# Softmax weights of eleven heads transposed by VectorE in 32x32 blocks by way of HBM, in place of TensorE

## The chip, the cores and the metric

One core of a Trainium2 chip. The time is device microseconds from the first to the last instruction of one launch, the median of several runs. Lower is better. TensorE is PE (its weight loads PEld), VectorE DVE, ScalarE ACT, GpSimd POOL, SyncE SP, whose queue issues most of the DMAs.

## The reference, cut to what matters

A block of an encoder on 256 tokens of width 2048: twelve attention heads beside a Fourier mixer, an output projection, and a gated feed-forward part, all in fp32.

```python
h = _rmsnorm(x, norm1_g)
proj = h @ w_in                       # q: 12 heads x 128, k and v: 4 x 128, u: 512
...
scores = jnp.einsum('bnqkgd,bnskd->bnkgqs', qb, kb).astype(jnp.float32)
scores = scores * (HEAD_DIM ** -0.5)
...
m = jnp.maximum(jnp.max(scores, axis=-1, keepdims=True), sink_b)
p = jnp.exp(scores - m)
p = p / (jnp.sum(p, axis=-1, keepdims=True) + jnp.exp(sink_b - m))
out = jnp.einsum('bnkgqs,bnskd->bnqkgd', p.astype(v.dtype), vb)
...
x = x + jnp.concatenate([a, f], axis=-1) @ w_out
x = x + _conv_ffn(_rmsnorm(x, norm2_g), w_up, dw_w, dw_b, w_down)
```

The sum over the keys `s` in the last einsum wants the softmax weights `p` with keys on the partitions. The scores come out with queries on the partitions. In between stands a transposition of 128 queries x 256 keys, twice (there are two blocks of 128 queries), for each head.

## The kernel before

**Units.** Weights arrive in units of 1 MB (128 partitions x 2048 fp32). Units 0 to 3 are the Fourier input, 4 to 7 the values (`v_hi`, `v_lo`), 8 to 23 the keys and queries in the order k0 q0 q1 q2 k1 q3 q4 q5 k2 ... (`QK_ORDER`), 24 to 39 the output projection, and then the feed-forward weights. Each fp32 operand is split into a rounded part and the rest (`hi`, `lo`), and a product is made of three matmuls hi x hi, lo x hi, hi x lo. So a weight is prepared by two instructions: ACT writes `hi` (`split`, L185), then DVE writes `lo` = raw - hi (L186).

**The order of the work** is written out by hand. Every engine runs its own queue in program order. A unit `i` issues, in this order: the small jobs listed in `before` (on PE, ahead of the projection), the projection of unit `i`, the jobs listed in `beside`, the split of unit `i + 2` with the load of unit `i + 5` on SP (the raw buffers are three, so a load waits until the split has freed one), and the jobs listed in `behind`. So on DVE and ACT the `beside` jobs of unit `i` stand between the split of unit `i + 1` and that of unit `i + 2`.

**A head through the units.** If query `h` is projected in unit `s`, then its sum leaves PSUM in `s + 1` (`qk_out`: ACT copies one half to `tmp`, DVE adds; `qk_parts`: ACT rounds into `qT`, DVE takes the rest). The scores are made by PE at the start of unit `s + 2` (`scores`), DVE adds the distance bias and finds the maximum (`scores_out`), and ACT takes the exponentials behind the split (`exps`). In `s + 3` DVE divides by the sums (`weigh`, L702 to L706). At the start of `s + 4` PE transposes four 128x128 blocks into PSUM (`turn`, L713), and ACT and DVE split the result into `pt0`, `pt1` (`turn_out`, L725, L726). At the start of `s + 5` PE multiplies by the values (`values`, L735), and `values_out` squares and scales the result into `cat` (`feature_out`, L492 and `split_scaled`, L234, L235), while POOL sums the squares.

Every fourth projection is a key, so in a round of four units each of these steps comes three times, and which unit lacks it depends on the step. The `beside` jobs of a unit before:

```python
        for kind, h in new:
            if kind == "q":
                at(beside, i, lambda k=kind, h=h: qk_out(k, h, st.pop(("ps", k, h))))
        if 4 in heads:
            at(beside, i, turn_out, heads[4])
        if 3 in heads:
            at(beside, i, weigh, heads[3])
```

and then the key's `qk_out`, `qk_parts`, `scores_out` and `values_out`. `heads[d]` is the head whose query was projected `d` units ago. In units 9 to 13 the four Fourier groups pass through the same engines (`fourier_channels` and what follows it); they use four buffers with the tag `sc`, which the scores take over.

Of the kernel before, what the change touches and what calls it, by code (L numbers as in the profile page):

```python
# [8 lines left out]
F32 = mybir.dt.float32  # L9
F32R = mybir.dt.float32r  # L10
AF = mybir.ActivationFunctionType
ALU = mybir.AluOpType

P = 128
D = 2048
S = 256
NK = D // P
HD = 128
NH = 12
# [32 lines left out]
N_OUT = N_QK + len(QK_ORDER)  # L52
# [44 lines left out]
def block_kernel(  # L97
# [18 lines left out]
    nc = tc.nc  # L116
# [4 lines left out]
    dram = ctx.enter_context(tc.tile_pool(name="dram", bufs=1, space=bass.MemoryType.DRAM))  # L121
    mm = ctx.enter_context(tc.tile_pool(name="mm", bufs=4, space=bass.MemoryType.PSUM))
    dn = ctx.enter_context(tc.tile_pool(name="dn", bufs=4, space=bass.MemoryType.PSUM))

    def f32(ap):
        return ap.bitcast(F32)
# [13 lines left out]
    def bank(pool, name):  # L140
        return pool.tile([P, 512], F32, tag=pool.name, name=name)
# [63 lines left out]
    for n, size in enumerate(U_LOADS[1:], 1):  # L205
        k = sum(U_LOADS[:n])
# [15 lines left out]
    ident = base.tile([P, P], F32, tag="ident", name="ident")  # L222
    make_identity(nc, ident)

    ps = bank(dn, "ps_warm")
# [21 lines left out]
    for c in range(4):  # L247
        t = base.tile([P, 4, 512], F32R, tag=f"hT{c}", name=f"hT{c}")
# [45 lines left out]
    k = 0  # L294
# [15 lines left out]
    ph = pa.enter_context(tc.tile_pool(name="pa", bufs=1))  # L310
# [103 lines left out]
    before, beside, behind = {}, {}, {}  # L414

    def at(when, i, f, *a):
        when.setdefault(i, []).append((f, a))
# [136 lines left out]

    def fourier_rows_out():
        for g in range(NG):
            t = ph.tile([P, 512], F32, tag="sc", name=f"uf{g}", bufs=4)[:, 0:S]
            if g % 2:
                nc.scalar.activation(t, held.pop(("f", g))[:, 0:S], AF.Copy)
            else:  # L560
                nc.vector.tensor_copy(t, held.pop(("f", g))[:, 0:S])
            us.append(t)
# [39 lines left out]
    at(beside, 8, fourier_weights_out)  # L602
    at(before, 7, fourier_rows)
    at(beside, 7, fourier_rows_out)
    at(beside, 8, lambda: rows_out(v_hi, v_lo, ps_v))
    at(behind, 8, distances)
# [23 lines left out]
    qk_sb, st = {}, {}  # L630
    sq_a = ph.tile([P, S], F32, tag="sq", name="sq_a")

    def qk_out(kind, h, ps):
        tmp = ph.tile([P, S], F32, tag="tmp", name=f"tmp_{kind}{h}", bufs=2)
        nc.scalar.activation(tmp, ps[:, S : 2 * S], AF.Copy)
        add = ph.tile([P, S], F32, tag="add", name=f"add_{kind}{h}", bufs=2)
        nc.vector.tensor_tensor(add, ps[:, 0:S], tmp, ALU.add)
        if kind == "k":
            nc.vector.tensor_tensor(add, add, r1b, ALU.mult)
        st["add", kind, h] = add  # L640
# [30 lines left out]
    def scores_out(h):  # L671

        ps = st.pop(("s", h))
        sc = ph.tile([P, 512], F32, tag="sc", name=f"sc{h}", bufs=4)
        mx = ph.tile([P, 2], F32, tag="mx", name=f"mx{h}", bufs=2)
        neg = ph.tile([P, 2], F32, tag="neg", name=f"neg{h}", bufs=2)
        for b in range(2):
            s = slice(b * S, (b + 1) * S)
            nc.vector.tensor_tensor_reduce(
                sc[:, s], ps[:, s], rel[:, s], -float(SL[h]), -3e38, ALU.add,  # L680
                ALU.max, mx[:, b : b + 1],
            )
        nc.vector.tensor_tensor(neg, mx, rq_neg, ALU.mult)
        nc.vector.tensor_scalar(neg, neg, sink_neg[:, h : h + 1], None, ALU.min)
        st["sc", h] = sc, neg
# [20 lines left out]
            nc.vector.tensor_scalar(sc[:, s], sc[:, s], ex[:, b : b + 1], None, ALU.mult)  # L706

    def turn(h):
        ps = st["t", h] = bank(dn, f"ps_t{h}")
        sc = st.pop(("sc", h))[0]  # L710
        for sb in range(2):
            for b in range(2):
                nc.tensor.transpose(  # L713
                    ps[:, b * S + sb * P : b * S + (sb + 1) * P],
                    sc[:, b * S + sb * P : b * S + (sb + 1) * P],
                    ident,
                )

    def turn_out(h):
        ps = st.pop(("t", h))  # L720
        pt = [
            ph.tile([P, 512], F32R, tag=f"pt{q}", name=f"pt{q}{h}", bufs=2)
            for q in range(2)
        ]
        nc.scalar.activation(pt[0], ps, AF.Copy)  # L725
        nc.vector.tensor_tensor(pt[1], ps, f32(pt[0]), ALU.subtract)  # L726
        st["p", h] = pt
# [21 lines left out]
    for i in range(N_QK, N_OUT + 8):  # L749
        heads = {i - s: h for (kind, h), s in slot_of.items() if kind == "q"}  # L750
        new = [kh for kh, s in slot_of.items() if i - s == 1]
        if i - 9 in range(NG):
            at(before, i, fourier_channels, i - 9)
        if 5 in heads:
            at(before, i, values, heads[5], mm if i < N_OUT else dn)
        if 4 in heads:
            at(before, i, turn, heads[4])
        if i == 15:
            at(before, i, total, sq_f, "f")
        if 2 in heads:  # L760
            at(before, i, scores, heads[2])

        for kind, h in new:
            if kind == "q":
                at(beside, i, lambda k=kind, h=h: qk_out(k, h, st.pop(("ps", k, h))))
        if 4 in heads:
            at(beside, i, turn_out, heads[4])
        if 3 in heads:
            at(beside, i, weigh, heads[3])
        for kind, h in new:  # L770
            if kind == "k":
                at(beside, i, lambda k=kind, h=h: qk_out(k, h, st.pop(("ps", k, h))))
            at(beside, i, qk_parts, kind, h)
        if 2 in heads:
            at(beside, i, scores_out, heads[2])
            at(behind, i, exps, heads[2])
        if 5 in heads:
            at(beside, i, values_out, heads[5])

    fourier_channels_steps()  # L780
    for n, (kind, h) in enumerate(QK_ORDER):
# [57 lines left out]
    for n, (c, kq) in enumerate(OUT_ORDER):  # L839
        i = N_OUT + n  # L840
# [14 lines left out]
        if kq >= 2:  # L855
            part = "a" if kq == 2 else "f"
            ps = ps_a[c] if kq < 3 else ps_a[c, "f"]
            last = c in added
# [306 lines left out]
    for q in range(2):  # L1165
        kind, j = items[q]
        ps = bank(mm, f"ps_{kind}{j}")
# [16 lines left out]
    for n, it in enumerate(items):  # L1184
# [8 lines left out]
        if it[0] in ("gate", "val"):  # L1193
            kind, j = it
            ps = bank(mm, f"ps_{kind}{j}")
# [4 lines left out]
        if it[0] == "product":  # L1200
            kind, g, c, p = it
            hi, lo = halves.pop(it)
            both = c == 2
            shape = (2, 1024) if both else (4, 512)
            for cc in (0, 1) if both else (c,):
                o = 512 * cc if both else 0
# [4 lines left out]
                ps = bank(mm, f"ps_{p}{g}{cc}")  # L1211
# [6 lines left out]
        else:  # L1218
            kind, g, c = it
            hi, lo = halves.pop(up_index[n])  # L1220
            ps = [bank(mm, f"ps_l{g}{c}{b}") for b in range(2)]
# [10 lines left out]
    i = up_index[n]  # L1232
# [156 lines left out]
```

## Time and profile before

| | |
|---|---|
| median of three runs | 905.73 us (905.62 to 905.91) |
| the profiled execution | 905.91 us, of which the span shown is 904.1 us |
| PE, PEld busy | 895.6 us, 808.5 us |
| DVE, ACT, POOL busy | 746.0 us, 546.7 us, 51.6 us |
| transposes of the softmax weights on PE (`ps_t`) | 48 matmuls of 128x128, 80.4 to 173.2 us |
| DMA | 214.86 MB, mean 238 GB/s |

The span is cut into instructions by engine. A timeline row reads: start in us, length in us, engine, line, operation, output <- inputs, partitions x elements and type, how many were joined into the row, and in brackets how long the engine had been idle and which instruction on which engine ended that. Names stand without their numbers. On PE, lengths overlap, because matmuls are pipelined: what one costs is read from the start of one to the start of the next. A row of the stretches view reads: the stretch, its length, then for each engine busy time and number of instructions, the granted clock of PE, the DMA engines' mean share and GB/s.

### The profile page before, as it was taken

The numbers are of one execution on the slowest core, as the hardware profiler recorded it, in microseconds if no ns is written. First come the engines' busy times: TensorE is split into PE (matmuls) and PEld (weight loads), VectorE is DVE, ScalarE is ACT, GpSimd is POOL, SyncE is SP. The second block draws the span as 40 slices with busy tenths as digits, with TensorE's granted clock in tenths as the row PEclk, the third lists the DMA queues.
The fourth block names the chain that finished last, engine by engine and source line by source line (L and its number), as shares of the span: only waits on it lengthen the run. The fifth ranks groups of instructions, "written<-read, shape, count | busy, mean of one in ns | idle before, by whom it ended". The sixth has DMA issues, their size and how long they took to land.

```text
span 904.1 us, 12736 instructions
## 1 busy us (share of the span) xinstructions
PE 895.6 (99%) x5064; PEld 808.5 (89%) x5064; DVE 746.0 (83%) x894; ACT 546.7 (60%) x661; POOL 51.6 (6%) x65
## 2 busy tenths in 40 slices
PE   9999999999999999999999999999999999999996
PEld 7899999888899999999999999999999999999885
DVE  7569888666668877889887998878988789998996
ACT  7757677555455656556565565566655566656544
POOL 0001111000000000000000000000000000000004
PEclk9999999999999999999999999999999999999999
DMA  9964544456568678677898779887888988779652
GB/s 359 343 232 142 187 155 171 145 182 227 192 242 272 231 242 252 187 256 235 271 265 271 245 258 285 261 278 238 274 250 244 312 263 263 242 240 289 213 198 94
DMA packets 32908, 214.86 MB, mean 238 GB/s; under 512 B 3632, under 2 KB 4016, under 8 KB 8528
## 3 DMA queue, kind: packets, MB, share of 16 engines
q1 hardware_dynamic: 28592, 184.29, 54.9%
q0 software_dynamic: 4112, 29.49, 17.5%
q8 instruction: 40, 0.66, 0.3%
q10 hardware_dynamic: 144, 0.26, 0.1%
q14 instruction: 20, 0.16, 0.0%
HBM read 211.93 MB, written 2.10 MB: 237 GB/s over the span
## 4 chain that ended last, share of the span: by engine, by line
PE 95%; DVE 2%; POOL 1%; issue 1%; ACT 0%; POOLq 0%; ACTq 0%; DVEq 0%
PE ps_val L395 17%; PE ps_gate L395 17%; PE ps_gate L397 8%; PE ps_val L397 8%; PE ps_q L395 5%; PE ps_P L1106 3%; PE ps_P L1108 3%; PE ps_P L1107 3%; PE ps_N L1106 2%; PE ps_N L1108 2%; PE ps_N L1107 2%; PE ps_u L289 2%; PE ps_q L397 2%; PE ps_a L378 2%; PE ps_a L380 2%; PE ps_a L379 2%
## 5 line engine op out<-in xcount | busy, mean ns | idle before, releaser
L186 DVE TENSOR_TENSOR parts<-raw,parts 128x2048 fp32r<-128x2048 f32 (+1 forms) x129 | 293.2, 2273 | 47.1 <-ACT parts L185 46.4
L185 ACT ACTIVATE parts<-raw 128x2048 fp32r<-128x2048 f32 (+1 forms) x129 | 245.6, 1903 | 44.5 <-PE ps_a L380 12.4
L395 PE MATMUL ps_val<-hU,parts 128*128 128x512 f32 x688 | 227.7, 382 | 0.0
L395 PE MATMUL ps_gate<-hU,parts 128*128 128x512 f32 x688 | 227.3, 382 | 0.0
L397 PE MATMUL ps_val<-hU,parts 128*128 128x256 f32 x688 | 187.5, 273 | 0.0
L397 PE MATMUL ps_gate<-hU,parts 128*128 128x256 f32 x688 | 186.9, 273 | 0.0
L395 PEld LDWEIGHTS ps_val<-hU,parts 128*128 128x128 f32 x688 | 130.0, 189 | 18.1
L395 PEld LDWEIGHTS ps_gate<-hU,parts 128*128 128x128 f32 x688 | 130.0, 189 | 18.1
L397 PEld LDWEIGHTS ps_val<-hU,parts 128*128 128x128 f32 x688 | 132.0, 192 | 0.8
L397 PEld LDWEIGHTS ps_gate<-hU,parts 128*128 128x128 f32 x688 | 131.8, 192 | 0.9
L884 ACT ACTIVATE ft_g<-ps_gate 128x256 f32<-128x256 f32 x43 | 16.5, 384 | 112.5 <-PE ps_gate L397 109.9
L395 PE MATMUL ps_q<-hT,parts 128*128 128x512 f32 x192 | 62.6, 384 | 0.0
L884 ACT ACTIVATE ft_v<-ps_val 128x256 f32<-128x256 f32 x43 | 16.5, 384 | 73.4 <-PE ps_val L397 73.4
L1106 PE MATMUL ps_P<-parts_P,op_P 128*128 128x512 f32 x144 | 54.7, 380 | 0.0
L1107 PE MATMUL ps_P<-parts_P,op_P 128*128 128x512 f32 x144 | 54.6, 379 | 0.0
L1108 PE MATMUL ps_P<-parts_P,op_P 128*128 128x512 f32 x144 | 54.6, 379 | 0.0
L397 PE MATMUL ps_q<-hT,parts 128*128 128x256 f32 x192 | 50.4, 273 | 0.0
L992 DVE TENSOR_TENSOR parts_N<-sumw,parts_N 128x2048 fp32r<-128x2048 f32 x18 | 41.2, 2288 | 9.9 <-ACT parts_N L991 9.9
L1106 PE MATMUL ps_N<-parts_N,op_N 128*128 128x512 f32 x108 | 41.0, 380 | 0.0
L1107 PE MATMUL ps_N<-parts_N,op_N 128*128 128x512 f32 x108 | 40.9, 379 | 0.0
L1108 PE MATMUL ps_N<-parts_N,op_N 128*128 128x512 f32 x108 | 40.9, 379 | 0.0
L395 PEld LDWEIGHTS ps_q<-hT,parts 128*128 128x128 f32 x192 | 36.1, 189 | 4.7
(344 smaller groups left out, 1555.0 us busy)
## 6 DMA issues: line engine op xcount, KB each, us to landing
raw<-in_w_up SPq DMA_DIRECT2D x86, 1024.0 KB, 6.2
raw<-in_w_in SPq DMA_DIRECT2D x20, 1024.0 KB, 4.9
sumw<-in_w_down POOLq DMA_DIRECT2D x18, 1024.0 KB, 8.4
raw<-in_w_out SPq DMA_DIRECT2D x16, 1024.0 KB, 4.8
raw<-in_w_down_late SPq DMA_DIRECT2D x4, 1024.0 KB, 5.3
u_raw<-in_u_in SPq DMA_DIRECT2D x4, 768.0 KB, 10.9
raw<-in_w_down_last SPq DMA_DIRECT2D x4, 768.0 KB, 4.2
u_raw<-in_u_in SPq DMA_DIRECT2D x7, 384.0 KB, 6.4
```

The costliest lines, as they stand in the source:

```text
L185: nc.scalar.activation(hi, raw, AF.Copy)
L186: nc.vector.tensor_tensor(lo, raw, f32(hi), ALU.subtract)
L289: nc.tensor.matmul(ps_u[b], block(hk(k), part, b, True), in_turn(w), start=k == 0 and n == 0, stop=k == NK - 1 and n == 2,)
L378: nc.tensor.matmul(ps, ah, wh, start=first and q == q0, stop=False)
L379: nc.tensor.matmul(ps, al, wh, start=False, stop=False)
L395: nc.tensor.matmul(ps, hi[:, s], in_turn(h), start=k == 0, stop=False)
L397: nc.tensor.matmul(ps[:, 0:S], lo[:, s], in_turn(h)[:, 0:P], start=False, stop=k == NK - 1)
L884: nc.scalar.activation(tmp, ps[:, S : 2 * S], AF.Copy)
L992: nc.vector.tensor_tensor(lo, src, f32(hi), ALU.subtract)
L1106: nc.tensor.matmul(ps, o[:, 0, p, :], wh, start=first and p == 0, stop=False)
L1107: nc.tensor.matmul(ps, o[:, 1, p, :], wh, start=False, stop=False)
L1108: nc.tensor.matmul(ps, o[:, 0, p, :], wl, start=False, stop=end)
```

## The change

Head 11 keeps its way. For heads 0 to 10 the four transposes on PE are replaced:

- `turn(h)`, now in unit `s + 3` directly behind `weigh(h)`: one DVE instruction transposes all 32x32 blocks of the 128x512 weights within their partitions' groups of 32, with the blocks regrouped in the output (`tb`); SP writes the result to a tensor in HBM.
- `fetch(h)`, in `s + 4`: four DMAs on SP read it back, each into 32 partitions, which brings every block to the partitions it belongs to (`td`).
- `turn_out(h)`, in `s + 5`, now the last of the `beside` jobs: ACT and DVE split `td` (in SBUF, not PSUM) into `pt0`, `pt1`.
- `values(h)` in `s + 6` and not `s + 5`.

`weigh` moves ahead of the query's `qk_out`. The buffers with the tag `sc` go from four to one; the room goes to `tb` (one) and `td` (two), and the Fourier groups' four buffers are spread over these.

```diff
-            t = ph.tile([P, 512], F32, tag="sc", name=f"uf{g}", bufs=4)[:, 0:S]
+            tag, bufs = [("sc", 1), ("tb", 1), ("td", 2), ("td", 2)][g]
+            t = ph.tile([P, 512], F32, tag=tag, name=f"uf{g}", bufs=bufs)[:, 0:S]
...
-        sc = ph.tile([P, 512], F32, tag="sc", name=f"sc{h}", bufs=4)
+        sc = ph.tile([P, 512], F32, tag="sc", name=f"sc{h}", bufs=1)
...
     def turn(h):
+        sc = st.pop(("sc", h))[0]
+        t = ph.tile([P, 512], F32, tag="tb", name=f"tb{h}", bufs=1)
+        nc.vector.transpose(
+            t.rearrange("p (k n e) -> p n k e", k=4, e=32),
+            sc.rearrange("p (n k e) -> p n k e", k=4, e=32),
+        )
+        st["h", h] = dram.tile([P, 512], F32, tag=f"turn{h}", name=f"turn{h}")
+        nc.sync.dma_start(st["h", h], t)
+
+    def fetch(h):
+        d = st["t", h] = ph.tile([P, 512], F32, tag="td", name=f"td{h}", bufs=2)
+        t = st.pop(("h", h))
+        for k in range(4):
+            nc.sync.dma_start(
+                d[32 * k : 32 * (k + 1), :].rearrange("r (a e) -> r a e", a=4),
+                t[:, P * k : P * (k + 1)].rearrange("(a r) e -> r a e", r=32),
+            )
+
+    def turn_out(h):
+        d = st.pop(("t", h)).rearrange("p (a n e) -> p n a e", a=4, e=32)
...
+        hi, lo = (t.rearrange("p (n a e) -> p n a e", a=4, e=32) for t in pt)
+        nc.scalar.activation(hi, d, AF.Copy)
+        nc.vector.tensor_tensor(lo, d, f32(hi), ALU.subtract)
...
-        if 5 in heads:
-            at(before, i, values, heads[5], mm if i < N_OUT else dn)
-        if 4 in heads:
-            at(before, i, turn, heads[4])
+        valued = [h for d, h in heads.items() if d == (5 if h == NH - 1 else 6)]
+        for h in valued:
+            at(before, i, values, h, mm if i < N_OUT else dn)
+        turned = {d: h for d, h in heads.items() if h < NH - 1}
+        last = {d: h for d, h in heads.items() if h == NH - 1}
...
+        if 4 in turned:
+            at(beside, i, fetch, turned[4])
+        if 3 in heads:
+            at(beside, i, weigh, heads[3])
+        if 3 in turned:
+            at(beside, i, turn, turned[3])
 
         for kind, h in new:
             if kind == "q":
                 at(beside, i, lambda k=kind, h=h: qk_out(k, h, st.pop(("ps", k, h))))
-        if 4 in heads:
-            at(beside, i, turn_out, heads[4])
-        if 3 in heads:
-            at(beside, i, weigh, heads[3])
...
-        if 5 in heads:
-            at(beside, i, values_out, heads[5])
+        for h in valued:
+            at(beside, i, values_out, h)
+        if 5 in turned:
+            at(beside, i, turn_out, turned[5])
```

How this stands in the engines' queues is shown for unit 18, in which query 6 is finished and head 5 weighed. The names carry their head or unit (the figures behind the underscore are buffer numbers). On DVE, from the split of unit 19 to that of unit 20, before:

```order
L186 TENSOR_TENSOR parts19_1249<-raw19_1005,parts19_1249 128x2048
L637 TENSOR_TENSOR add_q6_1306<-ps_q6_1193,tmp_q6_1304 128x256
L726 TENSOR_TENSOR pt14_1309<-ps_t4_1266,pt04_1308 128x512
L702 TENSOR_TENSOR sm5_1254<-sm5_1254,ex5_1255 128x2
L703 RECIPROCAL ex5_1255<-sm5_1254 128x2
L706 TENSOR_SCALAR sc5_1242<-sc5_1242,ex5_1255 128x256 x2
L235 SCALAR_TENSOR_TENSOR qT6_1316<-add_q6_1306,qT6_1316 128x256
L235 SCALAR_TENSOR_TENSOR cat3_1321<-ps_o3_1259,vec_88,cat3_1321 128x256
L186 TENSOR_TENSOR parts20_1325<-raw20_1093,parts20_1325 128x2048
```

and with the change:

```order
L186 TENSOR_TENSOR parts19_1265<-raw19_1002,parts19_1265 128x2048
L704 TENSOR_TENSOR sm5_1270<-sm5_1270,ex5_1271 128x2
L705 RECIPROCAL ex5_1271<-sm5_1270 128x2
L708 TENSOR_SCALAR sc5_1252<-sc5_1252,ex5_1271 128x256 x2
L715 STREAM_TRANSPOSE tb5_1317<-sc5_1252 128x4x4x32
L639 TENSOR_TENSOR add_q6_1323<-ps_q6_1198,tmp_q6_1321 128x256
L235 SCALAR_TENSOR_TENSOR qT6_1325<-add_q6_1323,qT6_1325 128x256
L740 TENSOR_TENSOR pt13_1329<-td3_1231,pt03_1328 128x512
L186 TENSOR_TENSOR parts20_1332<-raw20_1088,parts20_1332 128x2048
```

Weighing and the new transposition now stand ahead of the query's add, and the softmax parts, of head 3 and not head 4, have gone from behind the add to the place ahead of the next split. On ACT in the same unit, before:

```order
L635 ACTIVATE tmp_q6_1304<-ps_q6_1193 128x256
L725 ACTIVATE pt04_1308<-ps_t4_1266 128x512
L234 ACTIVATE qT6_1316<-add_q6_1306 128x256
L492 ACTIVATE sq3_1319<-ps_o3_1259 128x256
L234 ACTIVATE cat3_1321<-ps_o3_1259,vec_88 128x256
L185 ACTIVATE parts20_1325<-raw20_1093 128x2048
```

and with the change:

```order
L637 ACTIVATE tmp_q6_1321<-ps_q6_1198 128x256
L234 ACTIVATE qT6_1325<-add_q6_1323 128x256
L739 ACTIVATE pt03_1328<-td3_1231 128x512
L185 ACTIVATE parts20_1332<-raw20_1088 128x2048
L637 ACTIVATE tmp_q7_1389<-ps_q7_1275 128x256
```

ACT's half of the softmax parts (`pt0`) has moved from ahead of the query to between the query and the split. The values of head 3 are not in this unit any more; they are made a unit later. On SP, from the load of unit 21 to that of unit 24, where before there were only the loads:

```order
L177 DMA raw21_1177<-in_w_in 128x2048
L726 DMA td3_1231<-turn3_1148 32x4x128 x4
L720 DMA turn4_1242<-tb4_1240 128x512
L177 DMA raw22_1268<-in_w_in 128x2048
L726 DMA td4_1308<-turn4_1242 32x4x128 x4
L720 DMA turn5_1319<-tb5_1317 128x512
L177 DMA raw23_1335<-in_w_in 128x2048
L726 DMA td5_1384<-turn5_1319 32x4x128 x4
L177 DMA raw24_1416<-in_w_out 128x2048
```

Between two loads stand the four reads of one head and the write of the next.

More of the change, by code (lines that the diff above doesn't have):

```diff
@@ L708, in turn, with turn_last @@
     def turn(h):
+        sc = st.pop(("sc", h))[0]
[16 more added lines that the diff above has]
+        d = st.pop(("t", h)).rearrange("p (a n e) -> p n a e", a=4, e=32)
+        pt = [
+            ph.tile([P, 512], F32R, tag=f"pt{q}", name=f"pt{q}{h}", bufs=2)
+            for q in range(2)
+        ]
+        hi, lo = (t.rearrange("p (n a e) -> p n a e", a=4, e=32) for t in pt)
+        nc.scalar.activation(hi, d, AF.Copy)
+        nc.vector.tensor_tensor(lo, d, f32(hi), ALU.subtract)
+        st["p", h] = pt
+    def turn_last(h):
         ps = st["t", h] = bank(dn, f"ps_t{h}")
@@ L712, in turn, with turn_last_out @@
             for b in range(2):
[L713 to L719, printed above, removed]
+                o = b * S + sb * P
+                nc.tensor.transpose(ps[:, o : o + P], sc[:, o : o + P], ident)
+    def turn_last_out(h):
         ps = st.pop(("t", h))
@@ L753, in block_kernel @@
             at(before, i, fourier_channels, i - 9)
-        if 5 in heads:
-            at(before, i, values, heads[5], mm if i < N_OUT else dn)
-        if 4 in heads:
-            at(before, i, turn, heads[4])
+        valued = [h for d, h in heads.items() if d == (5 if h == NH - 1 else 6)]
[3 more added lines that the diff above has]
+        last = {d: h for d, h in heads.items() if h == NH - 1}
+        if 4 in last:
+            at(before, i, turn_last, last[4])
         if i == 15:
@@ L765, in block_kernel @@
                 at(beside, i, lambda k=kind, h=h: qk_out(k, h, st.pop(("ps", k, h))))
-        if 4 in heads:
-            at(beside, i, turn_out, heads[4])
-        if 3 in heads:
-            at(beside, i, weigh, heads[3])
+        if 4 in last:
+            at(beside, i, turn_last_out, last[4])
         for kind, h in new:
```

## The prediction

> **What bounds the kernel now.** I read the engine shares first, then the chain of work that ended last, then the waits of PE.
>
> ```profile
> PE 895.6 (99%) x5064; PEld 808.5 (89%) x5064; DVE 746.0 (83%) x894; ACT 546.7 (60%) x661; POOL 51.6 (6%) x65
> PE 95%; DVE 2%; POOL 1%; issue 1%; ACT 0%; POOLq 0%; ACTq 0%; DVEq 0%
> PE ps_warm L229 <- PEq L1379: 0.8, 1, 0.8
> ```
>
> PE is busy throughout, carries 95% of the chain, and waited once, at the start. So an instruction taken from PE is worth its whole length, and a wait put on PE costs its whole length. The change touches the units of queries and keys. The stretches view gives one round of four there, units 18 to 21 on PE. DVE and ACT finish in a unit what PE projected in the unit before, here three queries and a key.
>
> ```profile
> 113.47:139.76 26.29, 26.29 (x178) 24.61 (x177) 22.41 (x49) 18.71 (x37) 2.46 (x3) 1.00 0.46 160
> ```
>
> The round is 26.29 us, PE full, DVE busy 22.41, ACT 18.71, the granted clock 1.00.
>
> **What the change takes from PE.** The timeline of PE shows the units' first instructions.
>
> ```profile
> 93.08 0.39 PE L735 MATMUL ps_o<-pt,v_hi 128*128 128x256 f32 x2
> ...
> 113.47 0.39 PE L735 MATMUL ps_o<-pt,v_hi 128*128 128x256 f32 x2
> ...
> 114.14 0.60 PE L713 MATMUL ps_t<-ident,sc 128*128 128x128 f32 x4
> 114.50 1.33 PE L395 MATMUL ps_q<-hT,parts 128*128 128x512 f32 x5
> ...
> 159.65 0.60 PE L713 MATMUL ps_t<-ident,sc 128*128 128x128 f32 x4
> ```
>
> These are the starts of units 15, 18 (values of one head, transposes of another, then the projection) and 25. Matmuls overlap, so I cost them from start to start: four transposes hold PE 114.50 - 114.14 = 0.36 us, a head's values 114.14 - 113.47 = 0.67 us. Eleven heads lose their transposes: 11 x 0.36 = 4.0 us. That is the whole gain there can be.
>
> By shares it looks free. Three transposes on DVE, at about 0.7 us each, bring its 22.41 us to 24.5, below the 25.2 (26.29 - 3 x 0.36) that PE would need for a round. But DVE is not one pile of work: it hands work to ACT and back several times in a unit, and the change alters at which places.
>
> **What it costs on DVE and ACT.** The two timelines for units 16 (a query) and 17 (a key) of before, first DVE, then ACT:
>
> ```profile
> 99.89 2.29 DVE L186 TENSOR_TENSOR parts<-raw,parts 128x2048 fp32r<-128x2048 f32 x1 [0.37 <-ACT parts L185]
> 102.10 0.42 DVE L637 TENSOR_TENSOR add_q<-ps_q,tmp_q 128x256 f32<-128x256 f32 x1
> 102.43 0.15 DVE L702 TENSOR_TENSOR sm<-sm,ex 128x2 f32<-128x2 f32 x1
> ...
> 102.82 0.62 DVE L706 TENSOR_SCALAR sc<-sc,ex 128x256 f32<-128x256 f32 x2
> ...
> 105.59 2.29 DVE L186 TENSOR_TENSOR parts<-raw,parts 128x2048 fp32r<-128x2048 f32 x1 [0.26 <-ACT parts L185]
> ...
> 109.92 0.42 DVE L637 TENSOR_TENSOR add_k<-ps_k,tmp_k 128x256 f32<-128x256 f32 x1
> ...
> 111.72 0.83 DVE L653 TENSOR_TENSOR kT<-add_k,kT 128x256 fp32r<-128x256 f32 x1 [0.93 <-ACT kT L652]
> 112.47 0.41 DVE L679 CUSTOM_DVE_ANT_0 sc<-ps_s,rel 128x256 f32<-128x256 f32 x1
> ...
> 113.61 2.29 DVE L186 TENSOR_TENSOR parts<-raw,parts 128x2048 fp32r<-128x2048 f32 x1
> ```
>
> ```profile
> 102.55 0.56 ACT L234 ACTIVATE qT<-add_q 128x256 fp32r<-128x256 f32 x1 [1.08 <-DVE add_q L637]
> 103.01 0.37 ACT L492 ACTIVATE sq<-ps_o 128x256 f32<-128x256 f32 x1
> 103.27 0.47 ACT L234 ACTIVATE cat<-ps_o,vec 128x256 fp32r<-128x256 f32 x1
> 103.63 1.93 ACT L185 ACTIVATE parts<-raw 128x2048 fp32r<-128x2048 f32 x1
> ...
> 107.76 0.60 ACT L725 ACTIVATE pt<-ps_t 128x512 fp32r<-128x512 f32 x1 [0.87 <-PE ps_t L713]
> 108.26 0.38 ACT L635 ACTIVATE tmp_k<-ps_k 128x256 f32<-128x256 f32 x1
> 110.83 0.86 ACT L652 ACTIVATE kT<-add_k 128x256 fp32r<-128x256 f32 x1 [2.19 <-DVE add_k L639]
> 111.59 1.91 ACT L185 ACTIVATE parts<-raw 128x2048 fp32r<-128x2048 f32 x1
> ```
>
> The reader is to see a relay. DVE splits a weight (its half of the split), adds the query; ACT, which has waited for that add, rounds the query, squares and scales the values, and does its half of the next weight's split; only then can DVE begin the next split. From split to split in unit 16 that is 105.59 - 99.89 = 5.70 us, of which the weighing of the softmax (102.43 on) is not a part: it comes after the add, and lies beside ACT.
>
> The steps of the relay, from start to start: DVE's split 2.21 (99.89 to 102.10); add until ACT has it 0.45 (to 102.55); query on ACT 0.46; square and scaled values 0.62 (103.01 to 103.63); ACT's split until DVE has it 1.96 (to 105.59); the softmax parts on ACT 0.50 (107.76 to 108.26); for a key, add and scale 0.91 (109.92 to 110.83) and ACT's part 0.76 (to 111.59). Weighing takes from 102.43 until its last result is out, 102.82 + 0.62, and with a hand-over of 0.03, 1.04 us.
>
> The change puts weighing and transposition ahead of the add, and the softmax parts on ACT behind the values and ahead of the split. In the query units all three were beside the relay and are now in it; with a key, weighing stood ahead of the add before, too. The transposition has no row. The nearest is DVE's copy of the same shape in its softmax parts:
>
> ```profile
> 134.68 0.69 DVE L726 TENSOR_TENSOR pt<-ps_t,pt 128x512 fp32r<-128x512 f32 x1 [1.49 <-ACT pt L725]
> 135.29 0.15 DVE L702 TENSOR_TENSOR sm<-sm,ex 128x2 f32<-128x2 f32 x1
> ```
>
> 128x512 hold DVE 0.61 us from start to start. From below, the weighing's pair does 2 x 256 in 0.62, less an 0.09 tail, so 0.53; from above, the key's strided split does 256 in 0.75 (111.72 to 112.47), so 1.50 for 512. A gain is excluded, since nothing like it ran on DVE before. I take 0.61: same shape, one element after another. The row also shows the slack before: DVE idled 1.49 us there, for PE.
>
> The relay after the change, from split to split:
>
> - units 16, 20, 24 (query, weighing, values, softmax parts): 2.21 + 1.04 + 0.61 + 0.45 + 0.46 + 0.62 + 0.50 + 1.96 = 7.85
> - units 17, 21 (key, weighing, values): 2.21 + 1.04 + 0.61 + 0.91 + 0.76 + 0.62 + 1.96 = 8.11
> - units 18, 22 (query, weighing, softmax parts): 2.21 + 1.04 + 0.61 + 0.45 + 0.46 + 0.50 + 1.96 = 7.23
> - units 15, 19, 23 (query, values, softmax parts): 2.21 + 0.45 + 0.46 + 0.62 + 0.50 + 1.96 = 6.20
>
> A round takes 29.39 us, against 26.29 of PE before and 25.2 after. **The relay becomes the bound,** because PE cannot lag behind it: the softmax parts are now the last work of unit i ahead of the split, and the values, the first work of unit i + 1 on PE, need them. Behind the waiting values stand the scores and the whole projection.
>
> **The first stall.** In units 12 to 14 the last Fourier heads pass through DVE too.
>
> ```profile
> 72.57 2.29 DVE L186 TENSOR_TENSOR parts<-raw,parts 128x2048 fp32r<-128x2048 f32 x1
> 74.78 0.99 DVE L235 SCALAR_TENSOR_TENSOR cat<-y,vec,cat 128x256 fp32r<-128x256 f32 x1
> 75.68 0.41 DVE L637 TENSOR_TENSOR add_q<-ps_q,tmp_q 128x256 f32<-128x256 f32 x1
> ...
> 87.20 0.28 DVE L582 TENSOR_TENSOR y<-yh 128x127 f32<-128x127 f32 x1
> ...
> 87.67 2.29 DVE L186 TENSOR_TENSOR parts<-raw,parts 128x2048 fp32r<-128x2048 f32 x1
> ```
>
> Each such unit adds 0.90 (74.78 to 75.68) behind its split, and 0.47 (87.20 to 87.67) ahead of the next, or a copy on ACT that I take at the square's 0.26. The split at 72.57 still starts as before. Unit 12 then takes 2.21 + 0.90 + 1.04 + 0.61 + 0.45 + 0.46 + 0.26 + 1.96 = 7.89, to 80.46. Unit 13 goes by DVE alone: 2.21 + 0.90 + 1.04 + 0.61 + 0.91 + 0.89 (110.83 to 111.72) + 0.75 + 1.14 (112.47 to 113.61) + 0.47 = 8.92, to 89.38. In unit 14: 2.21 + 0.90 + 1.04 + 0.61 + 0.45 + 0.46 + 0.63 (ACT's softmax parts and hand-over) + 0.69 = 6.99; with another hand-over head 0's values start at 96.40. PE would be there at 93.08 - 2 x 0.36 - 0.67 (the values that unit 14 no longer holds) = 91.69. It waits 4.7 us.
>
> **The sum.** Unit 15 starts at 96.40; two rounds on, unit 23 at 96.40 + 2 x 29.39 = 155.18. From ACT's softmax parts in unit 22 to those in unit 24: 0.50 + 1.96 + 6.20 + (7.85 - 0.50 - 1.96) = 14.05, so unit 25 starts at 169.23; before, at 159.65. From there PE has one head's values more (0.67) and two heads' transposes fewer (0.72): -0.05. No query work is left, so no further wait. 169.23 - 159.65 - 0.05 = **+9.5 us**: 4.0 saved, 13.5 of waits. The profiled execution took 905.91 us with a span of 904.1, the median is 905.73; I put the sum on the median: **915.2 us**.
>
> **What I cost at nothing.** The DMAs: a head adds one write of 256 KB and four reads of 64 KB, on SP's queue, among the 1 MB weight loads.
>
> ```profile
> raw<-in_w_in SPq DMA_DIRECT2D x20, 1024.0 KB, 4.9
> out_y<-xs SPq DMA_DIRECT2D x8, 256.0 KB, 2.3
> DMA to landing us min/median/max: 11.2/11.2/11.2
> ```
>
> SP comes to a head's reads as soon as the split of the unit before has freed a weight buffer, right behind that load. The tightest reads are those of unit 18: they follow DVE's half of the split that starts unit 18's relay and lasts 2.29, and unit 19's softmax parts need them 7.23 + 3.74 (2.21 + 0.45 + 0.46 + 0.62) after its start. That leaves 8.7 us for load and reads; the rows say 4.9 + 2.3 = 7.2. If it were late, ACT would hold the split behind it. The write to HBM has a whole unit, and a load has three. The single score buffer costs nothing, since weighing, transposition and the next scores follow one another on DVE.
>
> **Rivals.**
>
> *The transposition is slow*, at the key's strided rate, 1.50: ten of them lie ahead of the last stall (heads 0 to 9), 10 x 0.89 = 8.9 more, 924.1 us. For it: the output is written in blocks out of order. Against: the innermost runs are 32 elements in a row. The Trainium skill, VectorE: DVE Perf Modes, section The three transpose paths, gives 311 ns for 128x128 in bf16 on VectorE (in blocks of 32) and 390 on TensorE, and the page's Rules for kernel authors prefer TensorE for 128x128 where PSUM will do. By that figure four side by side would be 1.24 us and the sum, an estimate, 921.5 us; the trace of before has no VectorE transposition to set beside it, and on TensorE one holds the queue 0.09 us here, not 0.39.
>
> *The transfers are late.* The last row is the landing of a small load that queued behind others at the start: 11.2 us. Were reads that slow, the two heads of a round with the least room (8.7 us, and 9.3 in unit 19: 6.20 + 5.39 - 2.29) would be 2.5 and 1.9 late: over two and a half rounds +11, 926 us. Against: little else moves here, 160 GB/s in the round's row.
>
> *PE stays the bound, and it is faster*: 905.7 - 4.0 = 901.8 us. It decides if the softmax parts are there when PE ends a unit, which takes a relay under 25.2 us a round. For it: the shares, 24.5 us of DVE. Against: the relay's sum, 4.2 us over.
>
> **How the numbers follow.** The forecast gets 0.80, the slow transposition 0.09, the late transfers 0.06, PE as the bound 0.05. The forecast's own range: the transposition at 0.53 takes 0.8 off; hand-overs at 0.05 in place of 0.03 add 0.02 some forty times, 0.8; the first stall's walk may err by 1.5 either way. With some way towards the slow transposition: 912 to 921.5. Changes of over 0.2% (1.8 us) can be told from none. Faster 0.04, same 0.02 (a relay between the two), slower 0.94.
>
> **What would show it.** Transposes into PSUM fall from 48 instructions to 4. In PE's waits stand the values, released by DVE's softmax parts, nine or so times and 13.5 us in all, the first near 4.7 us, then one of about 2.5 in each round. Units 15, 19 and 23 begin near 96.4, 125.8 and 155.2. ACT idles ahead of each query for DVE's add, about 2.7 us where it was 1.08 above. A DVE transposition takes 0.69. The forecast is wrong if PE shows no waits, if they go to a DMA, or if the stage's lengthening is in the transposition's own duration.

## The result, and the profile after

The changed kernel takes 915.42 us (median of 4, 914.93 to 915.61) against 905.82 us of the kernel before in the same session: ratio 1.0105, 95% interval 1.0088 to 1.0123. It is slower by 9.6 us; 915.2 was forecast. Engine shares, PE's granted clock in 40 slices, and the chain of work that ended last, of the changed kernel:

```profile
span 913.8 us, 12775 instructions
PE 896.7 (98%) x5020; PEld 808.9 (89%) x5020; DVE 753.5 (82%) x905; ACT 546.0 (60%) x661; POOL 53.2 (6%) x65
PEclk9999899999999999999999999999999999999999
PE 83%; DVE 8%; ACT 4%; issue 2%; DMA 1%; POOL 1%; ACTq 0%; POOLq 0%; DVEq 0%
```

PE did 44 matmuls fewer and lost 12 points of the chain: DVE and ACT now carry 12%. DVE's busy time rose by 7.5 us, about what eleven transpositions of 0.71 us make; its share of the span fell. Nothing in the engines' shares says that DVE is in the way. The waits of PE do (waiting group, released by; us in total, times, longest):

```profile
PE ps_o L768 <- ACT pt L739: 6.1, 3, 3.9
PE ps_o L768 <- DVE pt L740: 1.7, 3, 1.0
PE ps_warm L229 <- PEq L1421: 0.8, 1, 0.8
PE ps_u L289 <- ACT hT L234: 0.5, 1, 0.5
```

All new waits of any size are the values' (`ps_o`), for the softmax parts (`pt`), as in the forecast. The beginnings of units 15, 16, 19, 23 and 25 on PE:

```profile
95.64 1.31 PE L768 MATMUL ps_o<-pt,v_hi 128*128 128x256 f32 x2 [3.91 <-ACT pt L739]
...
105.74 0.39 PE L768 MATMUL ps_o<-pt,v_hi 128*128 128x256 f32 x2
...
124.78 0.38 PE L768 MATMUL ps_o<-pt,v_hi 128*128 128x256 f32 x1 [0.48 <-ACT pt L739]
125.51 0.38 PE L768 MATMUL ps_o<-pt,v_hi 128*128 128x256 f32 x1 [0.35 <-DVE pt L740]
...
153.91 0.38 PE L768 MATMUL ps_o<-pt,v_hi 128*128 128x256 f32 x1 [1.69 <-ACT pt L739]
154.64 0.38 PE L768 MATMUL ps_o<-pt,v_hi 128*128 128x256 f32 x1 [0.35 <-DVE pt L740]
...
169.40 0.39 PE L768 MATMUL ps_o<-pt,v_hi 128*128 128x256 f32 x2
```

The values start in two steps: the first matmul needs only ACT's part, the second waits for DVE's. Unit 25 begins 169.40 - 159.65 = 9.75 us later than before, and the spans differ by 913.8 - 904.1 = 9.7: after unit 25 nothing more is lost. The relay itself, DVE's half of each split (units 15 to 19 begin behind these rows), and the transposition with what follows it:

```profile
76.82 0.71 DVE L715 STREAM_TRANSPOSE tb<-sc 128x512 f32<-128x512 f32 x1
77.45 0.38 DVE L639 TENSOR_TENSOR add_q<-ps_q,tmp_q 128x256 f32<-128x256 f32 x1
...
97.42 2.29 DVE L186 TENSOR_TENSOR parts<-raw,parts 128x2048 fp32r<-128x2048 f32 x1 [1.11 <-ACT parts L185]
...
103.51 2.29 DVE L186 TENSOR_TENSOR parts<-raw,parts 128x2048 fp32r<-128x2048 f32 x1 [0.34 <-ACT parts L185]
...
111.34 2.29 DVE L186 TENSOR_TENSOR parts<-raw,parts 128x2048 fp32r<-128x2048 f32 x1 [0.35 <-ACT parts L185]
...
119.43 2.29 DVE L186 TENSOR_TENSOR parts<-raw,parts 128x2048 fp32r<-128x2048 f32 x1
...
126.58 2.29 DVE L186 TENSOR_TENSOR parts<-raw,parts 128x2048 fp32r<-128x2048 f32 x1 [1.12 <-DMA raw<-in_w_in]
```

From split to split: 6.09, 7.83, 8.09, 7.15; the round 126.58 - 97.42 = 29.16 us. (The last row's idle time is put down to a load. ACT's half of that split started at 124.63 and ran to 126.54, so it is the same hand-over as in the others.)

### The profile page after: what moved, and what is told of

Same layout as the page of the kernel before. It is cut to its first block, busy times and chain, and to the rows that moved or that the text cites. A ratio compares the mean times of both kernels' runs of the same rounds, so it can differ in the third digit from the quotient of the medians.

```text
span 913.8 us, 12775 instructions
## 1 busy us (share of the span) xinstructions
PE 896.7 (98%) x5020; PEld 808.9 (89%) x5020; DVE 753.5 (82%) x905; ACT 546.0 (60%) x661; POOL 53.2 (6%) x65
## 4 chain that ended last, share of the span: by engine, by line
PE 83%; DVE 8%; ACT 4%; issue 2%; DMA 1%; POOL 1%; ACTq 0%; POOLq 0%; DVEq 0%
PE ps_val L395 16%; PE ps_gate L395 16%; PE ps_gate L397 8%; PE ps_val L397 8%; DVE parts L186 4%; PE ps_P L1148 3%; PE ps_P L1149 3%; PE ps_P L1150 3%; PE ps_N L1148 2%; PE ps_N L1150 2%; PE ps_N L1149 2%; PE ps_u L289 2%; PE ps_a L379 2%; PE ps_a L378 2%; PE ps_a L380 2%
## 5 line engine op out<-in xcount | busy, mean ns | idle before, releaser
L395 PE MATMUL ps_q<-hT,parts 128*128 128x512 f32 x192 | 64.5, 393 | 0.0
```

Source lines behind the costliest of these rows:

```text
L395: nc.tensor.matmul(ps, hi[:, s], in_turn(h), start=k == 0, stop=False)
```

## The experiments

Each kernel ran beside the kernel before; times are medians, with the ratio to the kernel before and its 95% interval. The kernel before took 905.68 us beside the first four and 905.79 us beside the last three.

**Without the transposition.**

```diff
-        nc.vector.transpose(
-            t.rearrange("p (k n e) -> p n k e", k=4, e=32),
-            sc.rearrange("p (n k e) -> p n k e", k=4, e=32),
-        )
...
-        nc.sync.dma_start(st["h", h], t)
+        nc.sync.dma_start(st["h", h], sc)
```

> The changed kernel without the DVE transposition: SP writes the weighed scores to HBM as they are, so the softmax parts hold untransposed blocks; the write, the four reads and every other instruction stay, and the scores get two buffers. Relay (DVE and ACT hand work back and forth and set the pace): each of ten units on the path loses 0.63 us (transposition, start to start) and the 0.1 us until its input is out, so about 7 us less than the changed kernel's 915.4: 908 to 909.5. Transfers as the cause: unchanged, 915.

908.29 us, ratio 1.0028 (1.0018 to 1.0038): 7.1 us less than the change. One round of DVE's splits:

```profile
95.19 2.29 DVE L186 TENSOR_TENSOR parts<-raw,parts 128x2048 fp32r<-128x2048 f32 x1 [1.11 <-ACT parts L185]
...
122.26 2.29 DVE L186 TENSOR_TENSOR parts<-raw,parts 128x2048 fp32r<-128x2048 f32 x1 [1.11 <-ACT parts L185]
```

27.07 us against 29.16: 2.09 for three transpositions, 0.70 each. That is what it costs on the path, though DVE is busy for only 82% of the span. The second score buffer, which this kernel has because SP reads the scores themselves, is not the reason: in the change DVE never waited for the single one. And the kernel is still slower than before, though it gained PE's 4.0 us: what is left of the change costs more than that, and the next two kernels show that it is the order and not the transfers.

**Without the way through HBM.**

```diff
-        t = ph.tile([P, 512], F32, tag="tb", name=f"tb{h}", bufs=1)
+        t = ph.tile([P, 512], F32, tag="tb", name=f"tb{h}", bufs=3)
...
-        st["h", h] = dram.tile([P, 512], F32, tag=f"turn{h}", name=f"turn{h}")
-        nc.sync.dma_start(st["h", h], t)
+        st["t", h] = t
...
-        if 4 in turned:
-            at(beside, i, fetch, turned[4])
```

> The changed kernel without the way through HBM: ACT and DVE take the transposed blocks straight from the transposition's output (three buffers), so the blocks stay on the wrong partitions; no write, no reads. Relay: unchanged, 915 to 916, since no unit of the path waited for a read. Transfers as the cause (late reads, SP's queue, HBM traffic): falls by several us, to 910 or less.

915.17 us, ratio 1.0105 (1.0090 to 1.0120): the change's own time, 0.25 us apart with ranges that overlap. Fifty-five DMAs are gone and nothing is gained. The transfers lie wholly beside the path.

**The order alone, transposes on PE.**

```diff
+        if 3 in heads:
+            at(beside, i, weigh, heads[3])
         for kind, h in new:
             if kind == "q":
                 at(beside, i, lambda k=kind, h=h: qk_out(k, h, st.pop(("ps", k, h))))
-        if 4 in heads:
-            at(beside, i, turn_out, heads[4])
-        if 3 in heads:
-            at(beside, i, weigh, heads[3])
...
             at(beside, i, values_out, heads[5])
+        if 4 in heads:
+            at(beside, i, turn_out, heads[4])
```

> The kernel before, with its transposes on PE, but with the order of the changed kernel on DVE and ACT: weighing ahead of the query's add, the softmax parts last ahead of the split. No DVE transposition, no transfers, values not later. Relay: PE now waits for the softmax parts here too, about 4.5 us in all: 909.5 to 911. If transposition or transfers are the cause: unchanged, 905.8.

909.51 us, ratio 1.0042 (1.0025 to 1.0059). Not one operation differs from the kernel before, no buffer, no transfer; two jobs stand elsewhere in DVE's and ACT's queues, and 3.8 us are lost. Its waits of PE:

```profile
PE ps_o L735 <- DVE pt L726: 2.6, 4, 1.1
```

**The add ahead of weighing.**

```diff
         if 4 in turned:
             at(beside, i, fetch, turned[4])
+        for kind, h in new:
+            if kind == "q":
+                at(beside, i, lambda k=kind, h=h: qk_out(k, h, st.pop(("ps", k, h))))
         if 3 in heads:
             at(beside, i, weigh, heads[3])
         if 3 in turned:
             at(beside, i, turn, turned[3])
-        for kind, h in new:
-            if kind == "q":
-                at(beside, i, lambda k=kind, h=h: qk_out(k, h, st.pop(("ps", k, h))))
```

> The changed kernel with one move: the query's copy and add stand ahead of weighing and transposition again, which then lie beside ACT's rounding of the query. Relay: the query units lose up to 1.65 us each, the key units nothing; the stage falls by 6 to 7.5 us, to 908 to 909.5. DVE's total work as the bound: unchanged, 915.4, since DVE does the same instructions.

907.74 us, ratio 1.0027 (1.0017 to 1.0037), a little under the expected 908 to 909.5. The instructions are those of the change; moving the query's copy and add ahead of weighing and transposition gives back 7.7 of 9.6 us. DVE's amount of work is not the bound. PE still waits for the softmax parts, 4.4 us in four waits, at the beginnings of units 15, 19 and 23.

**The values a further unit later.**

```diff
-        valued = [h for d, h in heads.items() if d == (5 if h == NH - 1 else 6)]
+        valued = [h for d, h in heads.items() if d == (5 if h == NH - 1 else 6 if h > 8 else 7)]
```

> The changed kernel with the values of heads 0 to 8 one more unit later, so that PE need not have the softmax parts in the unit right after them. Relay: its round is still 29 us, PE is let go once and then waits for the query's parts at the scores instead; 914 to 916. If the place of the values alone were the cause: all waits go and 4.0 us are saved, about 902.

914.58 us, ratio 1.0097 (1.0083 to 1.0111). The waits only change their name:

```profile
PE ps_s L665 <- ACT qT L234: 6.5, 3, 3.1
PE ps_o L768 <- DVE pt L740: 0.9, 1, 0.9
```

The values wait only once more, for 0.9 us, and the scores wait for the query's parts instead, which stand earlier in the same relay. Its round:

```profile
97.05 2.29 DVE L186 TENSOR_TENSOR parts<-raw,parts 128x2048 fp32r<-128x2048 f32 x1 [1.11 <-ACT parts L185]
...
126.16 2.29 DVE L186 TENSOR_TENSOR parts<-raw,parts 128x2048 fp32r<-128x2048 f32 x1 [1.11 <-ACT parts L185]
```

29.11 us, as in the change. Slack in front of a consumer doesn't help when the producer's rate is the bound.

**PE kept busy through two waits.**

```diff
+    def keep_warm(i):
+        ps = bank(dn, f"ps_warm{i}")
+        for _ in range(12 if i == 15 else 6):
+            nc.tensor.matmul(ps, one, ones_512, start=True, stop=True)
...
+        if i in (15, 23):
+            at(before, i, keep_warm, i)
         for h in valued:
             at(before, i, values, h, mm if i < N_OUT else dn)
```

> The changed kernel with idle matmuls on constants ahead of the values in units 15 and 23 (12 and 6 of 128x512 in bf16), which fill the two waits after which the granted clock fell to 0.50. Relay: the clock stays at 1.00 there, yet the time stays, 915 to 915.8, since the next waits on the relay swallow what the slow clock cost. If the clock costs time of its own: about 5 us less, 910.

914.89 us, ratio 1.0100 (1.0086 to 1.0114). The stretches that hold unit 15 and unit 23 (the last three columns are clock, DMA share, GB/s):

```profile
95.00:104.00 9.00, 8.28 (x56) 7.66 (x57) 6.83 (x15) 6.58 (x11) 0.72 (x1) 1.00 0.63 217
152.00:163.00 11.00, 10.23 (x65) 8.52 (x64) 8.31 (x16) 7.99 (x15) 0.73 (x1) 1.00 0.76 255
```

The clock stayed at 1.00 in both, where the change has 0.65 and 0.84 in the mean of the same stretches (what the clock did there stands in the last section). The time is just under the expected 915 to 915.8 and 0.5 us below the change, with ranges that overlap. Where the time went is seen at unit 25, whose values now wait for DVE's softmax parts; in the change they did not wait there, and started at 169.40:

```profile
169.05 0.38 PE L768 MATMUL ps_o<-pt,v_hi 128*128 128x256 f32 x1 [1.05 <-DVE pt L740]
```

**The softmax parts and weighing behind the add.** Everything that DVE and ACT do beside the relay is put where one of them would wait for the other anyway. Heads 0, 10 and 11 keep PE's transposes: head 0 because the Fourier groups fill DVE there, 10 because its values were taken to come too late for the output projection (neither was tried otherwise). The scores of heads 0 and 11 go into the buffer `tb`.

```diff
-        valued = [h for d, h in heads.items() if d == (5 if h == NH - 1 else 6)]
+        valued = [h for d, h in heads.items() if d == (5 if h in ON_PE else 7)]
...
+        for kind, h in new:
+            at(beside, i, lambda k=kind, h=h: qk_out(k, h, st.pop(("ps", k, h))))
+        if 6 in turned:
+            at(beside, i, turn_out, turned[6])
         if 4 in turned:
             at(beside, i, fetch, turned[4])
+        if 4 in last:
+            at(beside, i, turn_last_out, last[4])
         if 3 in heads:
             at(beside, i, weigh, heads[3])
+        for kind, h in new:
+            at(beside, i, qk_parts, kind, h)
         if 3 in turned:
             at(beside, i, turn, turned[3])
...
-        if 5 in turned:
-            at(beside, i, turn_out, turned[5])
```

> Heads 1 to 9 by DVE and HBM, heads 0, 10 and 11 on PE as before; the query's or key's add comes first, then the softmax parts (a unit later than in the change, values later by one too), then weighing beside ACT's rounding, then the rest, then the transposition. Relay: a round falls below PE's 25.2 us, no waits are left, and nine heads save 0.36 us each: 3.2 less than before, 902.6. If DVE's load or the transfers bind: above 905.8.

903.14 us (902.74 to 903.86), ratio 0.9971 (0.9959 to 0.9983): faster than both kernels, 2.65 us below the one before. Its waits of PE, and a unit of DVE:

```profile
PE ps_s L665 <- DVE qT L235: 0.3, 1, 0.3
PE ps_s L665 <- ACT qT L234: 0.2, 1, 0.2
```

```profile
115.95 0.41 DVE L639 TENSOR_TENSOR add_q<-ps_q,tmp_q 128x256 f32<-128x256 f32 x1
...
116.66 0.62 DVE L708 TENSOR_SCALAR sc<-sc,ex 128x256 f32<-128x256 f32 x2
117.19 0.45 DVE L235 SCALAR_TENSOR_TENSOR qT<-add_q,qT 128x256 fp32r<-128x256 f32 x1
117.56 0.70 DVE L715 STREAM_TRANSPOSE tb<-sc 128x512 f32<-128x512 f32 x1
118.18 0.44 DVE L235 SCALAR_TENSOR_TENSOR cat<-ps_o,vec,cat 128x256 fp32r<-128x256 f32 x1
119.37 2.29 DVE L186 TENSOR_TENSOR parts<-raw,parts 128x2048 fp32r<-128x2048 f32 x1 [0.75 <-ACT parts L185]
```

Weighing lies where DVE, in the change, waited 0.6 us for ACT's rounded query (0.61 ahead of the query's rest at 108.39); the query's rest now follows it without a gap. The transposition fills the time in which ACT works towards its split, and in this unit DVE still waits 0.75 us for that. 3.2 us were expected, 2.65 came, and 0.5 of waits are left: one place, the scores at 142.90 us, where the query's parts come just late, first ACT's and then DVE's.

## Why the prediction was right

**The gain.** 44 transposes at 0.09 us, 4.0 us, was taken from PE's start-to-start times, and the last experiment shows that it is there: 0.36 us for each of nine heads is 3.2, of which 2.65 was seen with 0.5 of waits left.

**The relay** as the bound: the forecast gave 6.20, 7.85, 8.11 and 7.23 us from split to split, 29.39 a round; 6.09, 7.83, 8.09, 7.15 and 29.16 were measured. That it is this order, and not the amount of work, is shown by the order alone (+3.8 us with unchanged operations) and by the add put first (-7.7 us with unchanged operations). The pieces do not add up, since only what the relay takes beyond PE's own pace counts: the order alone sets 27.14 us a round (96.11 to 123.25) against PE's 26.29. That it is a rate, and not just the strict place of the values, is shown by the values put later (29.11 us a round, and 0.8 us gained).

**The transposition**: 0.61 us was taken from a copy of the same shape, 0.63 measured (76.82 to 77.45). Taking it out brought 7.1 us, 0.70 for each in a round. The slow rival (1.50) falls: 512 columns took 0.71 in all. The Trainium skill, VectorE: DVE Perf Modes, section The three transpose paths, has 311 ns for 128x128 in bf16; four times that, an estimate of 1.24 us, does not hold here, and the trace's row of the same shape was the better guide. The forecast also set 0.09 us against that section's 390 ns for TensorE; 0.09 is from start to start, and from start to end one transpose took 0.27 us in the trace of before, so the two need not measure the same thing.

**The transfers at nothing**: right, and shown by the kernel without them. Their duration was mis-sized. The reads were put at 2.3 us behind a load of 4.9, 7.2 in all within 8.7 of room; they landed after 4.9 (median), and the write, for which no time was worked out, after 4.4. First the write, then the reads:

```profile
DMA to landing us min/median/max: 2.9/4.4/5.3
DMA to landing us min/median/max: 4.2/4.9/5.5
```

Added as the forecast added them, load and reads are 9.8 us and too late. They were not, because the reads do not stand behind the load but run beside it. For the tightest ones SP issued them 0.40 us after the load, and ACT had no wait for them:

```profile
121.75 0.35 SPq L177 DMA_DIRECT2D raw<-in_w_in  x1
122.15 1.85 SPq L726 DMA_DIRECT2D td<-turn  x4
...
130.29 0.63 ACT L739 ACTIVATE pt<-td 128x512 fp32r<-128x512 f32 x1
```

So the term was right at nothing through two errors that cancel. ACT waited for reads twice, 3.4 us, for heads 9 and 10 at the stage's end, where DVE's half of the parts waited with it once, 2.1 us, and PE did not wait.

**The waits**: 13.5 us were forecast, in nine or so waits of the values; 7.8 are listed, in six. The sum was right and its form was not. The first (forecast 4.7, listed 3.91 to ACT's part) and the one in each round are there. But the sum's "13.5 of waits" left out that PE ran slowly behind two of the waits, so part of the loss stands in the projections, not in front of the values: unit 15 took 105.74 - 95.64 = 10.10 us, and unit 23, from 153.91 to 162.87, took 8.96, against 7.30 of unit 19 (124.78 to 132.08), which begins alike (unit 15 has four small matmuls more; with the clock kept it took 7.74). The rest is how a wait is listed: idle time runs from the modelled end of a 0.38 us matmul, while without a wait the next one starts 0.11 us after its start. That the slow clock cost next to no time of its own (0.5 us between the medians) is what the kernel kept busy says: relay and slow projection overlap. The wait of ACT for the query's add, forecast at about 2.7 us, was 1.4 to 2.9 us in these units.

**The first stall**: the softmax parts of head 0 were forecast for 96.37 and PE's arrival for 91.69; DVE ended them at 95.62 + 0.69 = 96.31. Units 19, 23 and 25 were forecast for 125.8, 155.2 and 169.23, and came at 125.51, 154.64 (second matmul of the values) and 169.40. Unit 25 began when PE was through unit 24, and the parts it needs were ready at 169.27: there the slow clock of unit 23 and the relay came out within 0.15 us of one another.

That the relay met 169.23 within 0.04 us is partly luck. Up to unit 23 it ran 0.6 us ahead of the forecast (154.58 against 155.18), since a round took 29.16 us and not 29.39. The last leg was forecast at 14.05 us and took 14.69, because it was followed on ACT alone: in unit 22 DVE's half of the softmax parts starts 0.64 us after ACT's, but in unit 24 it starts 1.46 us after, behind DVE's own work on the scores and the values. The two errors cancel.

```profile
167.12 0.63 ACT L739 ACTIVATE pt<-td 128x512 fp32r<-128x512 f32 x1
168.58 0.69 DVE L740 TENSOR_TENSOR pt<-td,pt 128x512 fp32r<-128x512 f32 x1
```

## What to carry to other kernels

Before an operation is moved to an engine with room, follow the hand-overs between the engines through one turn of the loop, and sum the path from one hand-over to the next: an engine that is busy 82% of the time, as DVE here, can be the bound if it and another wait for each other in turns. Put new work where its engine already waits for the other one, not ahead of what the other waits for. If a consumer waits, find out first if the producer is late or slow: more lead helps only against the first.

## What the hardware showed beside that

In the first wait the granted clock of PE fell. Stretches of the changed kernel, with the same columns:

```profile
94.00:95.00 1.00, 0.00 (x0) 0.00 (x0) 0.60 (x2) 0.36 (x2) 0.00 (x0) 0.73 0.96 393
95.00:96.00 1.00, 0.36 (x1) 0.29 (x1) 0.81 (x2) 1.00 (x3) 0.00 (x0) 0.50 1.02 394
98.00:99.00 1.00, 1.00 (x6) 1.00 (x6) 1.00 (x1) 0.00 (x0) 0.00 (x0) 0.50 0.02 6
102.00:103.00 1.00, 1.00 (x7) 0.91 (x7) 1.00 (x3) 1.00 (x1) 0.00 (x0) 1.00 0.93 393
...
157.00:158.00 1.00, 1.00 (x5) 0.82 (x4) 1.00 (x2) 0.00 (x0) 0.00 (x0) 0.50 0.17 53
```

It stood at 0.50 from within the 3.91 us of idle until between 101 and 102 us, and once more from 156 to 159 behind the waits of 1.69 and 0.35 us in unit 23. The Trainium skill, TensorE: Matmul & The Clock Gate, Part 1, says that the clock halves after an idle window of about 3.4 us, and that this window runs free of what the kernel does. Neither case agrees with that length, counted from the last projection's end. In the first, PE had idled since 91.73, and a mean of 0.73 between 94 and 95 us puts the fall, by estimate, near 94.5, after some 2.7 us. In the second only about 2.4 us lie between the last projection and the values' second half, and the clock fell near 155.9, by the same estimate (0.95 between 155 and 156 us), with PE at work again. That the window runs free of the kernel would fit with the next case, but no trace here shows the window. It is not fixed by the waits either. In the kernel without the way through HBM, PE waited as long at the same place, and the clock stayed:

```profile
153.98 0.38 PE L767 MATMUL ps_o<-pt,v_hi 128*128 128x256 f32 x1 [1.71 <-ACT pt L738]
```

```profile
157.00:158.00 1.00, 1.00 (x8) 0.92 (x7) 1.00 (x2) 0.00 (x0) 0.00 (x0) 1.00 0.00 0
```

Eight matmuls in a microsecond there, five in the change; and yet the two kernels differ by 0.25 us in time, since the relay sets the pace. What decides whether the clock falls after so short a wait was not tried.
